# Splitting weight chunks in one piece of 2048 columns instead of two of 1024, in a two-layer encoder trunk

## The chip, the cores and the metric

The kernel runs on one core of one Trainium2 chip. The metric is device time in microseconds for one execution. A core has TensorE (PE: matrix products), VectorE (DVE), ScalarE (ACT), GpSimd (POOL), and SyncE (SP), whose queue issues all DMA transfers here. Times of whole runs are medians; a trace comes from one profiled execution.

## The reference

The input x is 256 tokens of 2048 float32 values, with one conditioning vector c. Each of two layers has a token mixer and a SwiGLU feed-forward part, and each part is wrapped in the same frame:

```python
for layer in range(2):
    shift1, scale1, gate1, shift2, scale2, gate2 = split(silu(c) @ ada_w[layer] + ada_b[layer], 6)
    h = x * (1 + scale1) + shift1
    out = mixer_ab(h) if layer == 0 else mixer_cd(h)
    x = layer_norm(ALPHA * x + (1 + gate1) * out)
    h = x * (1 + scale2) + shift2
    x = layer_norm(ALPHA * x + (1 + gate2) * ((silu(h @ w_gate) * (h @ w_up)) @ w_down))
```

mixer_ab is a gated linear recurrence beside a spatial gating unit, mixer_cd is stick-breaking attention beside multi-scale pooling; both have one input projection (2048 to 4096 columns) and one output projection (2048 to 2048). The feed-forward width is 5632. The conditioning product silu(c) @ ada_w has 12,288 outputs a layer, each a dot product of length 2048. Nearly all of the work is products of 256 tokens with float32 weights that are read once.

## The kernel before

Weights come from memory as raw chunks of 1 MB: 128 partitions by four blocks of 512 columns, 2048 columns in all, where the four blocks are four slices of the contracted dimension. A chunk is split into a high part h (the value rounded to the product format) and a low part l (the rest): `split` (lines 81 to 86) lets ScalarE copy w into h (line 84) and VectorE subtract h from w into l (line 85). `load_w` (line 144) splits a chunk in two halves of 1024 columns. TensorE then computes, for each block of 512 columns, xh·h, xh·l and xl·h (lines 161 to 163, the function `products`): 24 products for a chunk with both groups of 128 tokens, 12 for a half. xh and xl are the same split of the activations.

The h pieces and the l pieces have pools of four buffers each (lines 52 and 53), so four halves, two chunks, exist at a time. A buffer can be written again when the last product that reads it is done. Raw chunks share a pool of four buffers (line 51) with the tiles of ada_w, also 1 MB each.

`linear` (line 181) runs a projection: for each group of output blocks, for each chunk of the contracted dimension, load, split, multiply, and at the last chunk evacuate the sums. After each chunk it calls a pump, which issues conditioning work at a rate: 1.0 ada_w tile a chunk up to and including part of the first feed-forward, then 0.65, 0.84 and 0.2. `ada_dot` (line 94) loads one tile of ada_w and lets VectorE multiply it with silu(c) and sum along the columns, 1024 columns at a time into two partial sums; `ada_final` (line 102) adds the two partial sums, adds the bias, and folds in norm weights.

In the program's head (lines 523 to 570) the input projection's first columns are made as the conditioning terms arrive: each of 16 steps needs two ada_w dot products before its products. The feed-forward of layer 0 starts with three passes that go through one chunk of the contracted dimension for ten output blocks each (rate 1.0, with an addition on VectorE for each output), so that the later quarters of its input can be conditioned meanwhile. At the end of each output or down projection a hand-off (`close`, line 326) follows: the last sums, the norm, and the first products of the next stage, in a written order.

Outside the hand-offs a scheduler places the instructions of each engine in a fixed order when the program is built. An engine works its queue strictly in that order.

Of the kernel before, what the change touches and what calls it, by code (L numbers as in the profile page):

```python
# [7 lines left out]
F32 = mybir.dt.float32  # L8
F32R = mybir.dt.float32r
AF = mybir.ActivationFunctionType  # L10
ALU = mybir.AluOpType
PSUM = bass.MemoryType.PSUM

P = 128
# [4 lines left out]
NB = 512  # L19
# [23 lines left out]
def trunk_kernel(ctx, tc, I, out):  # L43
    nc = tc.nc
    V, A, G, T = nc.vector, nc.scalar, nc.gpsimd, nc.tensor

    def pool(name, bufs, **kw):
        return ctx.enter_context(tc.tile_pool(name=name, bufs=bufs, **kw))

    const = pool("const", 1)  # L50
    p_raw = pool("raw", 4)
    p_h = pool("wh", 4)
    p_l = pool("wl", 4)
    p_xs = pool("xs", 4)
    p_res = pool("res", 1)
    p_row = pool("rows", 1)
    p_t = pool("tmp", 2)
    p_d = pool("dram", 2, space=bass.MemoryType.DRAM)

    silc = const.tile([P, D], F32, name="silc")  # L60
# [14 lines left out]
    def vc(name, i, n=1):  # L75
        a = _VEC[name][0] + i
        return vec[:, a:a + n]
# [3 lines left out]
    def split(src, hp, lp, shape, hname, lname):  # L81
        h = hp.tile(shape, F32R, name=hname)
        l = lp.tile(shape, F32R, name=lname)
        A.activation(h, src, AF.Copy)  # L84
        mark["v"] = V.tensor_tensor(l, src, h, op=ALU.subtract)  # L85
        return h, l
# [7 lines left out]
    def ada_dot(acc, l, idx, kb):  # L94
        w = p_raw.tile([P, D], F32, name="w")
        nc.sync.dma_start(w, I["ada_w"][l, idx, kb])
        for hf in range(2):
            cs = slice(hf * 1024, hf * 1024 + 1024)
            V.scalar_tensor_tensor(w[:, cs], w[:, cs], 1.0, silc[:, cs], op0=ALU.mult, op1=ALU.mult,  # L99
                                   accum_out=acc[:, hf:hf + 1])  # L100

    def ada_final(acc, l, s, nm, idx, k0, n):
        m = mods[l, s, nm][:, k0:k0 + n]
        V.tensor_tensor(m, acc[:, :, 0], acc[:, :, 1], op=ALU.add)
        bias = vc("ab", (6 * l + idx) * KB + k0, n)
        if nm == "sh":
            V.tensor_tensor(m, m, bias, op=ALU.add)
        else:
            V.scalar_tensor_tensor(m, m, 1.0, bias, op0=ALU.add, op1=ALU.add)
        ln = 2 * l + s - 1  # L110
        if nm == "sh" and ln >= 0:
            sc = mods[l, s, "sc"][:, k0:k0 + n]
            t4 = p_t.tile([P, n], F32, name="t4")
            V.tensor_tensor(t4, vc("nb", ln * 16 + k0, n), sc, op=ALU.mult)
            V.tensor_tensor(m, m, t4, op=ALU.add)
            V.tensor_tensor(sc, sc, vc("ng", ln * 16 + k0, n), op=ALU.mult)

    def ada_tiles(l, s, part, q, n=CH):
        for nm, idx in (("sc", 3 * s + 1), ("sh", 3 * s)) if part == "s" else (("gt", 3 * s + 2),):
            acc = p_t.tile([P, n, 2], F32, name="ga")  # L120
            for j in range(n):
                ada_dot(acc[:, j], l, idx, n * q + j)
                if j == n - 1:
                    ada_final(acc, l, s, nm, idx, n * q, n)
                yield

    def chain(units):
        for u in units:
            if callable(u):
                u()  # L130
            else:
                yield from ada_tiles(*u)
# [6 lines left out]
    def load_raw(src):  # L139
        w = p_raw.tile([P, 4, NB], F32, name="w")  # L140
        nc.sync.dma_start(w, src)
        return w

    def load_w(src):
        w = load_raw(src)
        return [split(w[:, 2 * hf:2 * hf + 2], p_h, p_l, [P, 2, NB], "h", "l") for hf in range(2)]

    def products32(bk, x, w, tb, halves, first, last):
        ts = slice(tb * P, tb * P + P)
# [31 lines left out]
    def linear(groups, chunks, wsrc, stat, evac, after=None, pump=None, opened=None, close=None,  # L181
# [3 lines left out]
        for gi, group in enumerate(groups):  # L185
            banks = opened if gi == 0 and opened is not None else {}
            for ci, ch in enumerate(chunks):
# [11 lines left out]
                if close is not None and left == 1:  # L199
                    close(group, {nb: load_w(wsrc(nb, ch)) for nb in group}, banks, st, evac)  # L200
                    break
                for nb in group:
                    xr = raw(gi, ci, nb) if raw is not None else None
                    hl = load_w(wsrc(nb, ch)) if xr is None else load_raw(wsrc(nb, ch))
                    flush(mark["v"])
                    for hf in range(2):
                        for tb in range(2):
                            if first and hf == 0:
                                banks[nb, tb] = acc_bank()
                            if xr is None:  # L210
                                products(banks[nb, tb], st, hl, tb, (hf,), first, last)
                            else:
                                products32(banks[nb, tb], xr, hl, tb, (hf,), first, last)
                    if last:
                        for tb in range(2):
                            evac(nb, tb, banks[nb, tb])
                    if pump is not None and not (close is not None and left <= QUIET):
                        pump()
# [277 lines left out]
    def mixer_ab(pump):  # L496
        with ExitStack() as st:
# [15 lines left out]
            with tc.tile_pool(name="pshead", bufs=1, space=PSUM) as p8, tc.tile_pool(name="hraw", bufs=3) as p_hr:  # L513
# [3 lines left out]
                def stream(nb, ch):  # L517
                    hl = load_w(src(nb, ch))
                    for tb in range(2):
                        bk = p8.tile([P, NB], F32, name=f"hs{tb}")  # L520
                        products(bk, xs[ch], hl, tb, range(2), True, True)
                        d = dst[nb][:, tb]
                        if ch == 0:
                            A.activation(d, bk, AF.Copy)
                        else:
                            V.tensor_tensor(d, d, bk, op=ALU.add)
                        if ch == 3:
                            A.activation(d, d, AF.Gelu_apprx_tanh)

                spread(silc, 4, lambda i: p8.tile([P, NB], F32, name=f"hs{i % 2}"), AF.Silu)  # L530
                for kb in range(KB):
                    ch, k = divmod(kb, CH)
                    xt = y[ch]
                    ada = ada_tiles(0, 0, "s", kb, 1)
                    if kb == 0:
                        drain(ada)
                    if kb == 4:
                        rate = lru_rate()
                    if k == 0:
                        nc.sync.dma_start(xt, I["xT"][:, 4 * ch:4 * ch + 4])  # L540
                    w = p_hr.tile([P, 3, NB], F32, name="w")
                    nc.sync.dma_start(w, I["w_hd"][kb])
                    drain(ada)
                    sc, sh = (mods[0, 0, n][:, kb:kb + 1] for n in ("sc", "sh"))
                    V.tensor_scalar(xt[:, k], xt[:, k], sc, sh, op0=ALU.mult, op1=ALU.add)  # L545
                    for i, (nb, tb) in enumerate(head):
                        T.matmul(banks[nb, tb], xt[:, k, tb * P:tb * P + P], w[:, i // 2], start=kb == 0, stop=kb == KB - 1)  # L547
                    if k == 3:
                        xs.append(xs_split(xt))
                    elif ch > 0:  # L550
                        stream((7, 4, 5)[k], ch - 1)
# [363 lines left out]
```

## Time and profile before

| what | value |
|---|---|
| timed runs | 2183.04 us median of 3 (2177.11 to 2186.82) |
| profiled execution, span from first to last instruction | 2175.9 us (the page gives no time beside the span) |
| TensorE busy | 2111.6 us, 97% |
| VectorE busy | 1618.6 us, 74% |
| ScalarE busy | 966.5 us, 44% |
| moved by DMA | 601.20 MB, mean 276 GB/s |

How to read it: an engine that is busy for most of the span is not at its peak for that reason, because a product's record is longer than the distance to the next one. Where engines work in a loop, the distance between starts is the cost of an instruction, and the record's length is the time until its result is there. The chain of waits says which work ended last at each step; only what lies in that chain can shorten the run.

### The profile page before, as it was taken

How to read it: one execution, taken by the hardware profiler on the slowest of the kernel's cores; microseconds unless marked ns; L12 is line 12 of the kernel's file. 1: busy time of each engine (PE TensorE's matmuls, PEld its weight loads, DVE VectorE, ACT ScalarE, POOL GpSimd, SP SyncE). 2: the span in 40 equal slices, each digit the busy share in tenths (PEclk: the TensorE clock that was granted, in tenths of full speed). 3: DMA queues.
4: the chain of work that ended last, by engine and by line, in shares of the span. 5: the costliest groups of instructions: out<-in, count | busy, mean ns of one | idle time of the engine just before them, and what ended most of it. 6: DMA issues, size and time to landing. Idle time of an engine off the chain costs nothing.

```text
span 2175.9 us, 24074 instructions
## 1 busy us (share of the span) xinstructions
PE 2111.6 (97%) x9124; PEld 1666.4 (77%) x9124; DVE 1618.6 (74%) x2202; ACT 966.5 (44%) x1124; POOL 31.5 (1%) x55
## 2 busy tenths in 40 slices
PE   7989999999999999999999999999999999999996
PEld 3556767887888888888868777868888888888885
DVE  7778988899977788889779977666555555555656
ACT  1215733544544445444444556354444444444442
POOL 0000000000000000000000011000000000000000
PEclk9999999999999999999999999999999999999998
DMA  9987787988888888888858877646676666555552
GB/s 399 388 322 267 303 329 297 341 325 336 301 314 312 322 330 322 335 319 312 319 217 311 324 267 292 261 173 221 230 271 229 222 226 233 208 203 193 194 194 91
DMA packets 84747, 601.20 MB, mean 276 GB/s; under 512 B 9444, under 2 KB 9876, under 8 KB 13846
## 3 DMA queue, kind: packets, MB, share of 16 engines
q1 hardware_dynamic: 84630, 599.67, 73.7%
q8 instruction: 71, 1.16, 0.2%
q14 instruction: 46, 0.37, 0.1%
HBM read 597.51 MB, written 2.12 MB: 276 GB/s over the span
## 4 chain that ended last, share of the span: by engine, by line
PE 85%; DVE 9%; ACT 2%; DMA 2%; issue 1%; POOL 1%; SPq 0%; DVEq 0%; ACTq 0%; POOLq 0%
PE acc L162 25%; PE acc L163 25%; PE acc L161 24%; DVE w L99 3%; PE hd L547 3%; PE acc L152 3%; DVE l L85 2%; PE aux L228 2%; DMA w<-in_ada_w 1%; PE hs L162 1%; PE hs L163 1%; PE hs L161 1%; DMA w<-in_w_cd 0%; ACT h L84 0%; POOL z L736 0%
## 5 line engine op out<-in xcount | busy, mean ns | idle before, releaser
L85 DVE TENSOR_TENSOR l<-w,h 128x1024 fp32r<-128x1024 f32 x676 | 822.9, 1223 | 421.4 <-ACT h L84 420.1
L84 ACT ACTIVATE h<-w 128x1024 fp32r<-128x1024 f32 x676 | 711.6, 1059 | 862.0 <-PE acc L163 689.4
L162 PE MATMUL acc<-l,xh 128*128 128x512 f32 x2608 | 1019.2, 391 | 6.2 <-DVE l L85 5.8
L161 PE MATMUL acc<-h,xh 128*128 128x512 f32 x2608 | 1018.2, 392 | 5.9 <-ACT xh L318 4.5
L163 PE MATMUL acc<-h,xl 128*128 128x512 f32 x2608 | 1018.3, 391 | 0.0
L162 PEld LDWEIGHTS acc<-l,xh 128*128 128x128 f32 x2608 | 489.8, 188 | 112.4 <-DVE l L85 11.8
L161 PEld LDWEIGHTS acc<-h,xh 128*128 128x128 f32 x2608 | 489.5, 188 | 108.2 <-ACT xh L318 5.5
L163 PEld LDWEIGHTS acc<-h,xl 128*128 128x128 f32 x2608 | 489.8, 188 | 100.4 <-DVE xl L319 0.3
L99 DVE SCALAR_TENSOR_TENSOR w<-w,silc 128x1024 f32<-128x1024 f32 x384 | 459.0, 1219 | 18.0 <-DMA w<-in_ada_w 15.6
L547 PE MATMUL hd<-w,y 128*128 128x512 f32 x192 | 93.8, 642 | 20.7 <-DVE y L545 20.7
L547 PEld LDWEIGHTS hd<-w,y 128*128 128x128 f32 x192 | 38.4, 205 | 72.7 <-issue 43.2
L85 DVE TENSOR_TENSOR xl<-hid,xh 128x1024 fp32r<-128x1024 f32 x44 | 53.9, 1224 | 34.2 <-ACT xh L84 33.6
L84 ACT ACTIVATE xh<-hid 128x1024 fp32r<-128x1024 f32 x44 | 46.8, 1063 | 63.0 <-PE acc L162 63.0
L152 PE MATMUL acc<-w,hx 128*128 128x512 f32 x96 | 43.1, 599 | 2.8 <-ACT hx L313 2.7
L161 PE MATMUL hs<-h,xh 128*128 128x512 f32 x96 | 40.9, 428 | 0.0
L162 PE MATMUL hs<-l,xh 128*128 128x512 f32 x96 | 39.0, 406 | 0.0
L163 PE MATMUL hs<-h,xl 128*128 128x512 f32 x96 | 38.0, 396 | 0.0
L84 ACT ACTIVATE xh<-y 128x1024 fp32r<-128x1024 f32 x12 | 12.7, 1058 | 56.6 <-DVE y L545 48.6
L152 PEld LDWEIGHTS acc<-w,hx 128*128 128x128 f32 x96 | 17.6, 190 | 23.4 <-issue 17.5
L99 DVE DVE_READ_ACCUMULATOR w<-w,silc 128x1 f32 x384 | 31.3, 82 | 0.0
L152 PE MATMUL acc<-w,y 128*128 128x512 f32 x64 | 28.5, 592 | 0.0
L427 DVE TENSOR_TENSOR hid<-hid,acc 128x512 f32<-128x512 f32 x40 | 27.2, 683 | 1.5 <-PE acc L163 1.4
(207 smaller groups left out, 851.4 us busy)
## 6 DMA issues: line engine op xcount, KB each, us to landing
w<-in_ada_w SPq DMA_DIRECT2D x192, 1024.0 KB, 5.1
w<-in_wg SPq DMA_DIRECT2D x88, 1024.0 KB, 5.2
w<-in_wu SPq DMA_DIRECT2D x88, 1024.0 KB, 5.1
w<-in_wd SPq DMA_DIRECT2D x88, 1024.0 KB, 4.9
w<-in_w_cd SPq DMA_DIRECT2D x32, 1024.0 KB, 6.2
w<-in_w_ab SPq DMA_DIRECT2D x20, 1024.0 KB, 5.2
w<-in_w_ab_out SPq DMA_DIRECT2D x16, 1024.0 KB, 7.0
w<-in_w_cd_out SPq DMA_DIRECT2D x16, 1024.0 KB, 6.7
```

The source lines that it names most:

```text
L84: A.activation(h, src, AF.Copy)
L85: mark["v"] = V.tensor_tensor(l, src, h, op=ALU.subtract)
L99: V.scalar_tensor_tensor(w[:, cs], w[:, cs], 1.0, silc[:, cs], op0=ALU.mult, op1=ALU.mult, accum_out=acc[:, hf:hf + 1])
L152: T.matmul(bk, x[:, k, ts], w[:, k], start=first and k == 0, stop=last and k == 3)
L161: T.matmul(bk, xh[:, k, ts], h[:, j], start=first and k == 0, stop=False)
L162: T.matmul(bk, xh[:, k, ts], l[:, j], start=False, stop=False)
L163: T.matmul(bk, xl[:, k, ts], h[:, j], start=False, stop=last and k == 3)
L228: T.transpose(pt[:, i], src[:, i * P:(i + 1) * P], ident)
L427: V.tensor_tensor(part(nb, tb), part(nb, tb), bk, op=ALU.add)
L547: T.matmul(banks[nb, tb], xt[:, k, tb * P:tb * P + P], w[:, i // 2], start=kb == 0, stop=kb == KB - 1)
```

## The change

The pools for h and l get two buffers each, and a buffer holds a whole chunk of 2048 columns. `load_w` splits a chunk in one call, so with one ScalarE copy and one VectorE subtraction of 2048 columns, and hands the two halves of the result to the same products as before. The memory used is the same. `ada_dot` is one VectorE instruction of 2048 columns with one sum, and `ada_final` no longer adds two partial sums.

```diff
-    p_h = pool("wh", 4)
-    p_l = pool("wl", 4)
+    p_h = pool("wh", 2)
+    p_l = pool("wl", 2)
...
-        for hf in range(2):
-            cs = slice(hf * 1024, hf * 1024 + 1024)
-            V.scalar_tensor_tensor(w[:, cs], w[:, cs], 1.0, silc[:, cs], op0=ALU.mult, op1=ALU.mult,
-                                   accum_out=acc[:, hf:hf + 1])
+        V.scalar_tensor_tensor(w, w, 1.0, silc, op0=ALU.mult, op1=ALU.mult, accum_out=acc)
...
-        V.tensor_tensor(m, acc[:, :, 0], acc[:, :, 1], op=ALU.add)
...
-            V.tensor_tensor(m, m, bias, op=ALU.add)
+            V.tensor_tensor(m, acc, bias, op=ALU.add)
...
-            V.scalar_tensor_tensor(m, m, 1.0, bias, op0=ALU.add, op1=ALU.add)
+            V.scalar_tensor_tensor(m, acc, 1.0, bias, op0=ALU.add, op1=ALU.add)
...
-            acc = p_t.tile([P, n, 2], F32, name="ga")
+            acc = p_t.tile([P, n], F32, name="ga")
...
-                ada_dot(acc[:, j], l, idx, n * q + j)
+                ada_dot(acc[:, j:j + 1], l, idx, n * q + j)
...
-        return [split(w[:, 2 * hf:2 * hf + 2], p_h, p_l, [P, 2, NB], "h", "l") for hf in range(2)]
+        h, l = split(w, p_h, p_l, [P, 4, NB], "h", "l")
+        return [(h[:, 2 * hf:2 * hf + 2], l[:, 2 * hf:2 * hf + 2]) for hf in range(2)]
```

The order of the instructions moves with it. First VectorE's queue in the input projection of layer 1, around chunks 177 to 180 of the 338 that are split, in the kernel before. L99 is a dot product, L85 a subtraction (l from w and h), L375 and L376 work on the residual x that is only due later, L104 and L109 finish a group of four dot products.

```order
L99 SCALAR_TENSOR_TENSOR w,ga<-w,silc 128x1024 x2
L375 TENSOR_TENSOR x<-x,rg 128x512
L104 TENSOR_TENSOR m11sc<-ga 128x4
L375 TENSOR_TENSOR x<-x,rg 128x512
L109 SCALAR_TENSOR_TENSOR m11sc<-m11sc,vec 128x4
L376 TENSOR_TENSOR x<-x,rb 128x512 x2
L85 TENSOR_TENSOR l<-w,h 128x1024 x2
L99 SCALAR_TENSOR_TENSOR w,ga<-w,silc 128x1024 x2
L375 TENSOR_TENSOR x<-x,rg 128x512 x2
L376 TENSOR_TENSOR x<-x,rb 128x512 x2
L85 TENSOR_TENSOR l<-w,h 128x1024 x2
```

Between two pairs of subtractions stand two dot products of 1024 columns with the residual additions of one chunk. The same place in the changed kernel, where lines behind the change are three lower (L372 and L373 are the residual work, L97 the dot product, L105 the first finishing step).

```order
L97 SCALAR_TENSOR_TENSOR w,ga<-w,silc 128x2048
L372 TENSOR_TENSOR x<-x,rg 128x512
L105 SCALAR_TENSOR_TENSOR m11sc<-ga,vec 128x4
L372 TENSOR_TENSOR x<-x,rg 128x512
L373 TENSOR_TENSOR x<-x,rb 128x512 x2
L85 TENSOR_TENSOR l<-w,h 128x2048
L97 SCALAR_TENSOR_TENSOR w,ga<-w,silc 128x2048
L372 TENSOR_TENSOR x<-x,rg 128x512 x2
L373 TENSOR_TENSOR x<-x,rb 128x512 x2
L85 TENSOR_TENSOR l<-w,h 128x2048
```

Each pair of 1024 wide instructions has become one of 2048, one small instruction is gone, and the sequence is the same.

Second, ScalarE's queue at the hand-off from the down projection of layer 0 to layer 1, in the kernel before. L84 is the copy of weights (h) or of hidden values (xh), L313 makes the scaled inputs hx and t of the next stage, L318 copies them.

```order
L84 ACTIVATE xh<-hid 128x1024
L84 ACTIVATE h<-w 128x1024 x17
L313 ACTIVATE hx_7814<-aux,m10sh,m10sc 128x128 x4
L313 ACTIVATE t_7843<-aux,m10sh,m10sc 128x128 x4
L318 ACTIVATE xh<-t_7843 128x4x128
```

Two of the 17 half copies make a chunk, so the odd one at the start closes a chunk begun above. The same place in the changed kernel (L310 and L315 are the scaled inputs and their copy).

```order
L84 ACTIVATE xh<-hid 128x1024
L84 ACTIVATE h<-w 128x2048 x9
L310 ACTIVATE hx_6962<-aux,m10sh,m10sc 128x128 x4
L310 ACTIVATE t_6991<-aux,m10sh,m10sc 128x128 x4
L315 ACTIVATE xh<-t_6991 128x4x128
```

Before, the last four of the 17 half copies belong to two chunks of the next stage; after, the last two of the 9 whole ones do. Both stand ahead of hx. SP's queue carries the same transfers; a few loads of norm rows, pooling weights and gate rows have changed places with their neighbours.

## Rows read from the trace of the kernel before

**Rows 1.** The page's head: span; busy us, share, instructions by engine.
```profile
span 2175.9 us, 24074 instructions
PE 2111.6 (97%) x9124; PEld 1666.4 (77%) x9124; DVE 1618.6 (74%) x2202; ACT 966.5 (44%) x1124; POOL 31.5 (1%) x55
```

**Rows 2.** Chain that ended last: the page's by engine, the view's own by line.
```profile
PE 85%; DVE 9%; ACT 2%; DMA 2%; issue 1%; POOL 1%; SPq 0%; DVEq 0%; ACTq 0%; POOLq 0%
by line: PE acc L162 24.6%; PE acc L163 24.5%; PE acc L161 24.3%; DVE w L99 3.2%; PE hd L547 3.0%; PE acc L152 2.9%; DVE l L85 2.4%; PE aux L228 1.9%; issue 1.5%; DMA w<-in_ada_w 1.2%; PE hs L162 0.9%; PE hs L163 0.9%; PE hs L161 0.9%; DMA 
```

**Rows 3.** Stretches: length, busy us (count) PE PEld DVE ACT POOL, clock, DMA.
```profile
1460.00:2156.00 696.00, 696.00 (x3113) 575.89 (x3112) 403.70 (x405) 308.80 (x314) 0.00 (x0) 1.00 0.59 212
```

**Rows 4.** Stretches, TensorE alone: length, busy us (instructions), clock, DMA.
```profile
520.00:530.00 10.00, 9.64 (x41) 1.00 0.94 367
1200.00:1210.00 10.00, 10.00 (x46) 1.00 0.94 338
```

**Rows 5.** Timeline, gate and up projection: start, length, engine, line, instruction, idle before.
```profile
1611.06 0.39 PE L161 MATMUL acc<-h,xh 128*128 128x512 f32 x1
...
1613.78 0.39 PE L161 MATMUL acc<-h,xh 128*128 128x512 f32 x1
1613.98 1.06 ACT L84 ACTIVATE h<-w 128x1024 fp32r<-128x1024 f32 x1 [1.66 <-PE acc L163]
...
1615.07 1.23 DVE L85 TENSOR_TENSOR l<-w,h 128x1024 fp32r<-128x1024 f32 x1 [1.50 <-ACT h L84]
```

**Rows 6.** Groups by shape: count, busy us, mean ns, idle before.
```profile
L319 DVE TENSOR_TENSOR xl<-t,xh 128x512 fp32r<-128x512 f32 x18 | 12.4, 688 | 20.2 <-ACT xh L318 20.1
...
L318 ACT ACTIVATE xh<-t 128x512 fp32r<-128x512 f32 x18 | 11.5, 640 | 0.2
```

**Rows 7.** The page's costliest groups: count, busy us, mean ns, idle before.
```profile
L85 DVE TENSOR_TENSOR l<-w,h 128x1024 fp32r<-128x1024 f32 x676 | 822.9, 1223 | 421.4 <-ACT h L84 420.1
L84 ACT ACTIVATE h<-w 128x1024 fp32r<-128x1024 f32 x676 | 711.6, 1059 | 862.0 <-PE acc L163 689.4
```

**Rows 8.** Timeline of VectorE in the head.
```profile
80.36 1.22 DVE L99 SCALAR_TENSOR_TENSOR w<-w,silc 128x1024 f32<-128x1024 f32 x1
...
81.50 1.22 DVE L99 SCALAR_TENSOR_TENSOR w<-w,silc 128x1024 f32<-128x1024 f32 x1
...
82.76 0.16 DVE L104 TENSOR_TENSOR m00sc<-ga 128x1 f32<-128x1 f32 x1
82.95 0.16 DVE L109 SCALAR_TENSOR_TENSOR m00sc<-m00sc,vec 128x1 f32<-128x1 f32 x1
```

**Rows 9.** Chain in the output projection of layer 0: start, us, what.
```profile
288.31 1.07 ACT h L84
...
290.68 0.50 PE acc L162
...
341.80 1.24 DVE l L85
```

**Rows 10.** Timeline of VectorE, layer 1.
```profile
1198.58 1.29 DVE L375 TENSOR_TENSOR x<-x,rg 128x512 f32<-128x512 f32 x2
```

**Rows 11.** Groups by shape, 1100 to 1300, TensorE.
```profile
L695 PE MATMUL aux<-pp,rg 128*128 128x256 f32 x32 | 7.4, 385 | 0.3 <-DVE pp L691 0.3
```

**Rows 12.** Timelines of ScalarE and TensorE at the second hand-off.
```profile
1105.15 1.06 ACT L84 ACTIVATE h<-w 128x1024 fp32r<-128x1024 f32 x1 [0.30 <-DVE x L269]
1106.12 1.49 ACT L313 ACTIVATE hx<-aux,m10sh,m10sc 128x128 f32<-128x128 f32 x4
...
1106.61 7.13 PE L152 MATMUL acc<-w,hx 128*128 128x512 f32 x16 [1.06 <-ACT hx L313]
```

**Rows 13.** Timelines of SP and ScalarE, output projection of layer 0.
```profile
291.79 0.33 SPq L141 DMA_DIRECT2D w<-in_w_ab_out  x1
...
302.69 0.33 SPq L141 DMA_DIRECT2D w<-in_w_ab_out  x1
...
299.21 2.01 ACT L84 ACTIVATE h<-w 128x1024 fp32r<-128x1024 f32 x2 [2.83 <-DMA w<-in_w_ab_out]
```

## The prediction

> **What bounds the kernel now.** I read the page's busy shares first, then the chain of waits, then stretches of TensorE, then single loops. TensorE is busy nearly all of the 2175.9 us span, VectorE three quarters, ScalarE under half [rows 1]. The chain that ended last runs 85% through TensorE and 9% through VectorE [rows 2]. In the longest stretch, 1460 to 2156, TensorE has no idle at all [rows 3]: a saving on VectorE or ScalarE is worth nothing there. At full pace TensorE starts 46 matmuls in 10 us (1200 to 1210), and in the worst 10 us of the middle stage 41 [rows 4]. So the change can gain only where VectorE stands in the chain: the head, the stage up to 365, and short pieces after it. Everywhere else the question is whether it makes TensorE wait. The clock that the profile grants is 1.00 in these stretches, so it is no term.
>
> **The loop that the change alters.** Twelve matmuls, one half of a chunk, take 1613.78 - 1611.06 = 2.72 us, a chunk 5.44. ScalarE starts the next copy 0.20 after TensorE has gone on to the next half (1613.98), the copy takes 1.06, VectorE's subtraction starts 0.03 later and takes 1.23: done 2.52 after the half was given back [rows 5]. Before, with four half buffers, this half is wanted three halves later, 8.16 us, and its low part only with the second matmul, 0.23 later: about 5.8 us to spare.
>
> After, a buffer comes back only when the whole chunk is done, and is wanted one chunk later. No 2048 wide instruction stands in the trace, so I bound it. From the 512 wide rows [rows 6] and the 1024 wide ones [rows 7], one doubling more gives 1.06 + 2 x (1.06 - 0.64) = 1.90 on ScalarE and 1.22 + 2 x (1.22 - 0.69) = 2.29 on VectorE; at most they cost two of the old ones, 2.12 and 2.45. I take 1.90 and 2.29, since the same kind of instruction gives both points of the line. Done at 0.20 + 1.90 + 0.03 + 2.29 + 0.05 = 4.47, wanted at 5.67: 1.2 us to spare (0.8 at the upper bound). So no chunk waits by itself, but the reserve against bursts falls from 5.8 to 1.2.
>
> **What is saved.** On VectorE two old dot products start 1.14 apart (80.36, 81.50), and the sum of the two halves costs 0.19 until the next small instruction (82.76 to 82.95) [rows 8]. One 2048 wide instruction holds VectorE 1.14 + 2 x 0.54 = 2.22 where two held 2.28: 0.06 a pair, for 338 splits and 192 dot products 32 us, and some 80 sums at 0.19 (one per accumulator group) 15 us. Of the 1619 us of VectorE only what lies in the chain counts. Bounds: nothing, and the saving on all that the chain holds, 3.2% of the span in dot products (70 us, 30 pairs, at 0.25 each 7.6) and 2.4% in subtractions (52 us, 23 pairs, 1.4) [rows 2]: 9 us.
>
> **Sum, stage by stage.**
> Head (to 200 us): each step of the first projection needs two dot products and their sums one after the other, 0.5 us less a step. About seven of the sixteen steps have TensorE waiting for them (four at the start, three where a group of four ends, counted in the chain): -3.5.
>
> 200 to 365: transfers pace the weights. When TensorE is already waiting, the halves no longer overlap: at 288.31 the copy starts, and TensorE goes on at 290.68 [rows 9]; with the whole chunk it needs 1.90 + 2.29 + 0.09 = 4.28 instead of 2.37: +1.9. The piece of the chain on VectorE that ends with the subtraction at 341.80 [rows 9] costs another 1.1 at its end, and its 13 merged pairs give back 1: +2 together.
>
> Middle (365 to 690): VectorE must do a split, a dot product and two additions a chunk. Two 512 wide additions start 0.60 apart (1.29 for two) [rows 10]. Before 2.28 + 2.28 + 1.20 = 5.76, after 2.22 + 2.22 + 1.20 = 5.64, against TensorE's 5.44; only eight chunks of ten have a dot product. Before loses little, 5 starts of 46 in the worst slice [rows 4]; after is 0.12 cheaper a chunk but has less reserve. With the two later places where four residual instructions meet a dot product: +1.
>
> 1165 to 1420: the two orders shown for VectorE carry the same work. Between two splits it may hold 5.44 - 2.22 = 3.22 without loss, and 1.2 in all may pile up. The intervals in a row are 2.40 + 2.22 = 4.62, then 2.40, then 4.77 (0.15 for a small one), then 4.62: 0.2 lost, 0.4 left over, then 0.75 and 1.4 lost: +2.35. Before, the same four sum to about 4 us over, under its 5.8, and [rows 4] shows 46 starts there. The two intervals behind, with the pooling, are longer (6.2 and 7.2), but TensorE has the pooling matmuls (16 of a group of 32 with 7.4 us [rows 11]) and sixteen transposes there, so I count 1.3 for its waits, and 0.85 for the attention: +4.5.
>
> Hand-offs: at 1105.15 ScalarE starts its last half copy, at 1106.12 the scaled inputs, and TensorE goes on at 1106.61 [rows 12]. The order after keeps both copies ahead; the second is released by the same matmul but takes 1.90: +0.85, at two of the three hand-offs: +1.7.
>
> Stages that TensorE fills, and the tail: 0. The cover is the 1.2 us; in the down projection a copy of hidden values as long as an old half copy, about 1 us, stands ahead of the split, in the gate projection one activation. At the upper bound of the 2048 wide costs the first would lose 0.1 a chunk pair, 5 us in all; below zero nothing can come here, as TensorE has no idle. SP issues the same transfers, and the moved row loads change places with others that wait for buffers anyway.
>
> Sum: -3.5 + 2 + 1 + 4.5 + 1.7 = +5.7 on 2175.9, so 2182. The page gives no other time for its execution; the median of the timed runs lies 7.1 above the span, so I predict 2189.
>
> **Rivals.**
> Faster, because VectorE's chain is worth its whole saving and no burst reaches TensorE: -9, so 2174. For it: VectorE stands in the chain for 9% of the span, 196 us. Against: the 85% on TensorE [rows 2].
>
> Slower, by the lost reserve. The place is VectorE's queue, where a split stands behind a burst; it decides from 1.2 us over 3.22 a chunk. If TensorE's own extra work does not hide the bursts between 1165 and 1420 they cost about 12, the middle 5, the hidden copies of the down projections 5, the stage to 365 2, hand-offs 1.7, less 3.5 for the head: +22, so 2205. For it: bursts of 4.6 and more follow each other in the order. Against: they fall where pooling and attention fill TensorE. The Trainium skill, Perfetto Trace Analysis, section Optimizing Scalar/DVE Operations, sides with it: larger operations help when the engine is saturated, but "If Scalar/Vector aren't saturated, but are causing bubbles on other engines, breaking up instructions may allow work to be completed sooner." VectorE is at 74% and the copy at 288.31 fits that rule; a reader of the rule alone would take the 2205.
>
> Slower, by the transfers. A raw buffer is given back later. In the loop issued at 291.79, landed at 299.21, issued again at 302.69 [rows 13] the part after landing is 3.48; whole it is 1.90 + 2.29 + 0.06 = 4.25: 0.39 a chunk, if the loop of four raw buffers binds. With two loads a chunk in about 46 chunks that is 18, with the other terms but the 2 of the stage to 365 +22, again 2205. For it: the copy at 299.21 had waited 2.83 us for its transfer [rows 13]. Against: a load that queues less lands sooner, so part of it comes back.
>
> **How the numbers follow.** Forecast 0.45, faster rival 0.15, lost reserve 0.25, transfers 0.15. A change under 0.5%, 11 us, can't be told from none, so faster is under 2172, slower over 2194. Faster: under half of its rival and a little of the forecast, 0.14. Slower: nine tenths of the two slow rivals and the upper end of the forecast, 0.40. Same: 0.46. The forecast's own range is 2178 to 2200; the range with the rivals 2171 to 2213.
>
> **What would show it.** After: splits of about 1.90 and 2.29; TensorE without idle from 1460 on; new idle behind the subtraction between 1165 and 1240, 3 to 6 us in all; the hand-offs later by under 1 us each; the head 3 us shorter. I am wrong if TensorE waits for the subtraction in stretches where VectorE has time, if ScalarE's waits for transfers turn into idle of TensorE by the chunk, or if the 2048 wide instructions lie outside their bounds.

## The result

The changed kernel takes 2210.15 us (median of 4 runs, 2206.69 to 2212.84) against 2180.4 of the kernel before in the same session: a ratio of 1.013, 95% interval 1.0111 to 1.0149. It is 1.3% slower. The time lies inside the range of 2171 to 2213, but the likeliest case, 2189 with its own range of 2178 to 2200, did not come; nearest are the two slow rivals, the lost reserve and the transfers, both priced at 2205. Of the three outcomes, slower (chance 0.40) came and not same (0.46).

The page after: span and engines, the chain, the costliest groups (answering to [rows 1, 2, 7]).

```profile
span 2204.9 us, 22580 instructions
PE 2119.9 (96%) x9124; PEld 1667.9 (76%) x9124; DVE 1569.0 (71%) x1417; ACT 898.9 (41%) x777; POOL 35.9 (2%) x55
...
PE 83%; DVE 9%; ACT 3%; DMA 3%; issue 2%; POOL 1%; DVEq 0%; POOLq 0%; ACTq 0%
...
L85 DVE TENSOR_TENSOR l<-w,h 128x2048 fp32r<-128x2048 f32 x338 | 774.3, 2291 | 420.2 <-ACT h L84 419.5
...
L84 ACT ACTIVATE h<-w 128x2048 fp32r<-128x2048 f32 x338 | 647.4, 1915 | 802.1 <-PE acc L160 685.8
...
L97 DVE SCALAR_TENSOR_TENSOR w<-w,silc 128x2048 f32<-128x2048 f32 x192 | 438.9, 2287 | 52.8 <-DMA w<-in_ada_w 49.3
```

VectorE is busy for 50 us less and ScalarE for 68 us less, and the run is longer. The prices are those estimated: 1.915 for the copy (1.90), 2.291 for the subtraction (2.29). What failed is where they were set against the need of TensorE.

**Where the 29 us arise.** TensorE has 9124 products and transposes in each trace, so the start of the n-th in one can be set against the start of the n-th in the other. The two orders differ in at least 857 places, but at every stage's end in the table below the n-th product is the same one in both. The table gives how much later each stage of the changed kernel ends than it did before, less what it was already late when the stage began.

| stage, by the times of before | us | forecast |
|---|---|---|
| head, to 200 | -3.7 | -3.5 |
| output projection of layer 0, to 350 | +3.6 | +2 (to 365) |
| first hand-off, 350 to 400 | +8.7 | 0.85 at two of the three hand-offs |
| feed-forward of layer 0, 400 to 1090 | +7.3 | +1, residual included |
| second hand-off, 1090 to 1150 | +4.1 | as the first |
| input projection, attention, 1150 to 1404 | +2.9 | +4.5 |
| third hand-off, 1404 to 1465 | +4.1 | as the first |
| feed-forward of layer 1, 1465 to 2140 | +0.4 | 0 |
| last chunks, 2140 to the end | +1.7 | 0 |

The three hand-offs and the last chunks make 18.5 of the 29.0, where 1.7 was forecast.

**The hand-off.** First TensorE in the kernel before, at the first two products of the second of the last two chunks; then TensorE, ScalarE and VectorE of the changed kernel at the same place, the second hand-off.

```profile
1096.79 0.39 PE L161 MATMUL acc<-h,xh 128*128 128x512 f32 x1
1097.02 0.39 PE L162 MATMUL acc<-l,xh 128*128 128x512 f32 x1
```

```profile
1109.71 0.39 PE L160 MATMUL acc<-h,xl 128*128 128x512 f32 x1
1109.94 0.39 PE L158 MATMUL acc<-h,xh 128*128 128x512 f32 x1
...
1112.66 0.39 PE L158 MATMUL acc<-h,xh 128*128 128x512 f32 x1
1114.43 0.50 PE L159 MATMUL acc<-l,xh 128*128 128x512 f32 x1 [1.39 <-DVE l L85]
```
```profile
1110.14 1.92 ACT L84 ACTIVATE h<-w 128x2048 fp32r<-128x2048 f32 x1 [3.52 <-PE acc L160]
...
1122.70 1.91 ACT L84 ACTIVATE h<-w 128x2048 fp32r<-128x2048 f32 x1 [0.81 <-PE acc L160]
1124.52 1.49 ACT L310 ACTIVATE hx<-aux,m10sh,m10sc 128x128 f32<-128x128 f32 x4
```
```profile
1112.09 2.29 DVE L85 TENSOR_TENSOR l<-w,h 128x2048 fp32r<-128x2048 f32 x1 [3.15 <-ACT h L84]
```

The chunk ahead of the last two ends with the product at 1109.71 and frees its buffers; at 1109.94 the first of the two begins. But `close` (line 326) takes the two last chunks by token group: twelve products of one, then twelve of the other. So the second, which goes into the freed buffers, is wanted after 12 x 0.2267 = 2.72 us, its low part after 2.95, and not after 5.67 as in the body of a projection. Its buffer needs 0.20 + 1.92 + 0.03 + 2.29 + 0.05 = 4.49: late by 1.54. Measured against the pitch (0.2267 a product): 1114.43 instead of 1112.89, 1.54. Before, the same product started without a wait (1097.02). The same wait of 1.39 idle stands at all four places (358.02, 1114.43, 1435.65, 2180.32); at the last pair of chunks it stands in the stretch that answers to [rows 3], where TensorE had no idle: there TensorE now has 696.00 - 694.61 = 1.39 idle.

```profile
1488.00:2184.00 696.00, 694.61 (x3104) 573.62 (x3103) 393.92 (x255) 276.70 (x177) 0.00 (x0) 1.00 0.58 212
```

The forecast term of the hand-offs is there as it was worked out: hx starts behind a 1.91 copy, and TensorE goes on after 1.91 idle where [rows 12] show 1.06: 0.85, at the second and the third.

```profile
1125.02 7.13 PE L149 MATMUL acc<-w,hx 128*128 128x512 f32 x16 [1.91 <-ACT hx L310]
...
1446.24 7.13 PE L149 MATMUL acc<-w,hx 128*128 128x512 f32 x16 [1.91 <-ACT hx L310]
```

**The first hand-off** loses more. VectorE there, before and after, then TensorE after:

```profile
371.03 0.26 DVE L289 BATCH_NORM_AGGREGATE mv<-st 128x2 f32<-128x24 f32 x1
371.33 0.15 DVE L291 TENSOR_SCALAR rs<-mv 128x1 f32<-128x1 f32 x1
```
```profile
374.84 0.26 DVE L286 BATCH_NORM_AGGREGATE mv<-st 128x2 f32<-128x24 f32 x1
375.01 2.23 DVE L97 SCALAR_TENSOR_TENSOR w<-w,silc 128x2048 f32<-128x2048 f32 x1
...
377.17 0.15 DVE L288 TENSOR_SCALAR rs<-mv 128x1 f32<-128x1 f32 x1
```
```profile
378.74 1.94 PE L225 MATMUL aux<-ident,x 128*128 128x128 f32 x8 [3.50 <-DVE x L301]
```

The scheduler has put a whole dot product between the aggregate of the norm and its next step, rs, at both token groups (363.24 and 375.01). Before, two half dot products stood in the second norm too, but ahead of its last statistics, and none in the first. This stands in the changed order of instructions and I did not look there: I had compared the hand-off on ScalarE alone.

**The clock.** In the first profile of before TensorE's granted clock is at its full level (2.4 GHz) from 181 us to 2164. In the changed kernel it falls to one half (1.2 GHz) in the stretches below, each behind idle at a hand-off (and once at 319); the same products then start 0.43 apart instead of 0.23.

```profile
377.40:384.20 6.80, 5.46 (x13) 3.33 (x14) 3.28 (x7) 2.54 (x6) 0.55 (x1) 0.50 0.61 255
1135.20:1138.50 3.30, 3.30 (x11) 2.69 (x10) 2.05 (x4) 0.06 (x1) 0.00 (x0) 0.50 0.55 231
1456.00:1459.30 3.30, 3.23 (x9) 2.55 (x10) 1.61 (x3) 0.01 (x1) 0.00 (x0) 0.50 0.00 0
```

At the second hand-off the products in that stretch lose 0.2 each, with the transposes 1.6 in all. There 1.54 + 0.85 + 1.6 = 4.0 of the 4.1. At the first hand-off the longer stretch costs 2.3.

**The middle.** TensorE's waits for the subtraction between the first two hand-offs, before and after (us in total, times, longest).

```profile
PE acc L162 <- DVE l L85: 0.8, 3, 0.4
```
```profile
PE acc L159 <- DVE l L85: 5.9, 5, 2.6
```

The longest of the five: VectorE in the feed-forward of layer 0, then TensorE.

```profile
708.85 2.29 DVE L97 SCALAR_TENSOR_TENSOR w<-w,silc 128x2048 f32<-128x2048 f32 x1 [5.17 <-DMA w<-in_ada_w]
...
711.07 4.49 DVE L85 TENSOR_TENSOR l<-w,h 128x2048 fp32r<-128x2048 f32 x2
```
```profile
713.41 0.50 PE L159 MATMUL acc<-l,xh 128*128 128x512 f32 x1 [2.62 <-DVE l L85]
```

VectorE waits 5.17 us for an ada_w tile while a split, its copy long done, stands behind the dot product. One more of the five (0.2 at 665.77) is of this kind. The other three (0.7 at 480.75, 1.2 at 531.74, 1.2 at 560.53; 3.1 together) are of another: there the split stands behind an addition of the three passes, and the addition waits for TensorE's own sums. VectorE, then TensorE:

```profile
528.79 0.69 DVE L424 TENSOR_TENSOR hid<-hid,acc 128x512 f32<-128x512 f32 x1 [1.18 <-PE acc L160]
529.39 2.29 DVE L85 TENSOR_TENSOR l<-w,h 128x2048 fp32r<-128x2048 f32 x1
```
```profile
531.74 0.50 PE L159 MATMUL acc<-l,xh 128*128 128x512 f32 x1 [1.17 <-DVE l L85]
```

The tiles do come later for VectorE than before: its dot products wait for them 49.3 us in the whole run, where they waited 15.6 in the first profile of before and 25.3 in the second (below).

```profile
DVE w L99 <- DMA w<-in_ada_w: 15.6, 18, 3.6
```
```profile
DVE w L97 <- DMA w<-in_ada_w: 49.3, 36, 7.4
```

### The profile page after: what moved, and what is told of

Read it like the earlier page. It is cut to its first block, busy times and chain, and to the rows that moved or that the text cites. A ratio compares the mean times of both kernels' runs of the same rounds, so it can differ in the third digit from the quotient of the medians.

```text
span 2204.9 us, 22580 instructions
## 1 busy us (share of the span) xinstructions
PE 2119.9 (96%) x9124; PEld 1667.9 (76%) x9124; DVE 1569.0 (71%) x1417; ACT 898.9 (41%) x777; POOL 35.9 (2%) x55
## 4 chain that ended last, share of the span: by engine, by line
PE 83%; DVE 9%; ACT 3%; DMA 3%; issue 2%; POOL 1%; DVEq 0%; POOLq 0%; ACTq 0%
PE acc L159 24%; PE acc L160 24%; PE acc L158 24%; DVE l L85 3%; DVE w L97 2%; PE hd L544 2%; PE acc L149 2%; PE aux L225 2%; DMA w<-in_ada_w 1%; ACT h L84 1%; PE hs L159 1%; PE hs L160 1%; PE hs L158 1%; DMA w<-in_w_ab_out 1%; POOL th L733 1%
## 5 line engine op out<-in xcount | busy, mean ns | idle before, releaser
L85 DVE TENSOR_TENSOR l<-w,h 128x2048 fp32r<-128x2048 f32 x338 | 774.3, 2291 | 420.2 <-ACT h L84 419.5
L84 ACT ACTIVATE h<-w 128x2048 fp32r<-128x2048 f32 x338 | 647.4, 1915 | 802.1 <-PE acc L160 685.8
L97 DVE SCALAR_TENSOR_TENSOR w<-w,silc 128x2048 f32<-128x2048 f32 x192 | 438.9, 2287 | 52.8 <-DMA w<-in_ada_w 49.3
L84 ACT ACTIVATE xh<-hid 128x1024 fp32r<-128x1024 f32 x44 | 46.8, 1063 | 144.5 <-PE acc L159 144.5
L85 DVE TENSOR_TENSOR xl<-hid,xh 128x1024 fp32r<-128x1024 f32 x44 | 53.9, 1224 | 53.1 <-ACT xh L84 53.1
L395 ACT ACTIVATE sg<-acc 128x512 f32<-128x512 f32 x34 | 20.4, 600 | 46.9 <-PE acc L160 46.9
L149 PEld LDWEIGHTS acc<-w,hx 128*128 128x128 f32 x96 | 18.4, 198 | 25.9 <-issue 18.5
L84 ACT ACTIVATE xh<-y 128x1024 fp32r<-128x1024 f32 x12 | 12.7, 1058 | 53.4 <-DVE y L542 44.0
L316 DVE TENSOR_TENSOR xl<-t,xh 128x512 fp32r<-128x512 f32 x18 | 12.4, 689 | 27.0 <-ACT xh L315 27.0
```

Source lines behind the costliest of these rows:

```text
L97: V.scalar_tensor_tensor(w, w, 1.0, silc, op0=ALU.mult, op1=ALU.mult, accum_out=acc)
L149: T.matmul(bk, x[:, k, ts], w[:, k], start=first and k == 0, stop=last and k == 3)
L395: A.activation(sg, bk, AF.Silu)
```

## The experiments

All edits are to the changed kernel unless the text says otherwise. Lags are against the first profile of before, by stage as above. Every edit also changes the order that the scheduler makes, so the total of a run tests an edit together with its order; a wait at one place can be followed by itself.

**The kernel before, once more.** No edit.

> The kernel before, profiled once more. Theory: whether the granted clock falls behind the waits of a hand-off varies from execution to execution, so this one has one to three half-speed stretches between 200 and 2150 us, each worth 1.4 to 1.7 us at the hand-offs, and a span of 2177 to 2183. Rival (the changed kernel's longer waits alone make the clock fall): none, as in the first profile, and a span within 1 us of 2175.9 there.

Measured: span 2181.7, one half-speed stretch behind the second hand-off.

```profile
1121.40:1124.80 3.40, 3.40 (x11) 2.73 (x10) 2.75 (x5) 0.99 (x3) 0.00 (x0) 0.50 0.12 51
```

It loses 1.4 there, with the waits that the first profile had. So a fall behind a hand-off is partly chance, and the clock is no clean part of the 29. The first profile was a fortunate one: a run takes some 1.8 more than its span (2183.39 and 2181.7 here, 2206.69 and 2204.9 after), so its 2175.9 lies 2 to 5 us under the medians of before (2180.1 to 2183.04 less 1.8), and the 7.1 that I put between span and time was mostly that. This execution is also 1.8 later at 200 us, so the head's 3.7 is uncertain by as much or more.

**Only the dot products wide.**

```diff
-    p_h = pool("wh", 2)
-    p_l = pool("wl", 2)
+    p_h = pool("wh", 4)
+    p_l = pool("wl", 4)
...
-        h, l = split(w, p_h, p_l, [P, 4, NB], "h", "l")
-        return [(h[:, 2 * hf:2 * hf + 2], l[:, 2 * hf:2 * hf + 2]) for hf in range(2)]
+        return [split(w[:, 2 * hf:2 * hf + 2], p_h, p_l, [P, 2, NB], "h", "l") for hf in range(2)]
```

> Only the dot products are 2048 wide; splits as before (1024 wide, four half buffers). Theory (the loss is made by the whole-chunk splits at the hand-offs): the head keeps its 3.7 us, the hand-offs stand as before, so 2 to 5 us under the kernel before, 2175 to 2179. Rival (wide dot products stand ahead of the splits on VectorE and hold them up): 5 to 15 us over before.

Measured: 2183.17, ratio 1.0008 (0.9998 to 1.0018). Neither: no loss, and no gain. The head is 4.7 ahead at 200 us; 3.3 is given back between 400 and 1090 (2.5 of it between 640 and 800) and 4.4 between 1150 and 1404, and two half-speed stretches behind hand-offs take 3.1. The wide dot product alone does not explain the result.

**Only the splits wide.** The other half of the change: `ada_dot` and `ada_final` as in the kernel before.

> Only the splits are 2048 wide with two whole buffers; dot products as before, 1024 wide in two sums. Theory: the loss at the hand-offs stays and the head gives nothing back, so 24 to 33 us over before, 2204 to 2213; idle of 1.39 on TensorE before the low product of the second of the last two chunks, four times. Rival (wide dot products): at most 15 us over before.

Measured: 2214.84, ratio 1.0147 (1.0126 to 1.0168): 32 over before, within the 24 to 33 expected; the four waits are there. With the splits alone the loss is as large, though not at the same places: the first hand-off costs 1.7 instead of 8.7 (one half dot product stands between the aggregate and rs of the first norm, none in the second), and the stage to 350 and the middle lose more.

**The same buffers, filled in two instructions.**

```diff
-        h, l = split(w, p_h, p_l, [P, 4, NB], "h", "l")
-        return [(h[:, 2 * hf:2 * hf + 2], l[:, 2 * hf:2 * hf + 2]) for hf in range(2)]
+        h = p_h.tile([P, 4, NB], F32R, name="h")
+        l = p_l.tile([P, 4, NB], F32R, name="l")
+        hl = [(h[:, 2 * hf:2 * hf + 2], l[:, 2 * hf:2 * hf + 2]) for hf in range(2)]
+        for hf in range(2):
+            s = w[:, 2 * hf:2 * hf + 2]
+            A.activation(hl[hf][0], s, AF.Copy)
+            mark["v"] = V.tensor_tensor(hl[hf][1], s, hl[hf][0], op=ALU.subtract)
+        return hl
```

> Whole-chunk buffers, two each as in the changed kernel, but filled by two 1024 wide instructions on each engine; dot products 2048 wide. Theory (a whole buffer is harmless if its first half is ready 2.6 us after release instead of 4.5, since the hand-off wants it after 2.95): no 1.39 idle at the hand-offs, no fall of the granted clock behind them, 3 us under to 5 over before, 2177 to 2185. Rival (that a whole buffer comes back late is enough by itself): 15 to 25 over before.

Measured: 2183.08, ratio 1.0004 (0.9993 to 1.0016). Two whole buffers instead of four halves cost nothing that can be measured; the 27 us between this kernel and the changed one go with the width of the instructions that fill them. No idle at the four places. (One expectation missed: a half-speed stretch follows at the second hand-off all the same, with the waits of before: chance again.) The rule that I had set beside the rival holds here: the Trainium skill, Perfetto Trace Analysis, section Optimizing Scalar/DVE Operations, says that where VectorE or ScalarE is not saturated but makes others wait, breaking up its instructions may let work complete sooner. VectorE is at 71%, and halving brings the whole loss back.

**One copy, two subtractions; two copies, one subtraction.**

```diff
-        for hf in range(2):
-            s = w[:, 2 * hf:2 * hf + 2]
-            A.activation(hl[hf][0], s, AF.Copy)
-            mark["v"] = V.tensor_tensor(hl[hf][1], s, hl[hf][0], op=ALU.subtract)
+        A.activation(h, w, AF.Copy)
+        for hf in range(2):
+            mark["v"] = V.tensor_tensor(hl[hf][1], w[:, 2 * hf:2 * hf + 2], hl[hf][0], op=ALU.subtract)
```
```diff
+        for hf in range(2):
+            A.activation(hl[hf][0], w[:, 2 * hf:2 * hf + 2], AF.Copy)
+        mark["v"] = V.tensor_tensor(l, w, h, op=ALU.subtract)
```

(both against the kernel with two instructions; the second replaces the same loop)

> The changed kernel with one 2048 wide copy on ScalarE and two 1024 wide subtractions on VectorE for a chunk. Theory (the time from the release of a whole buffer to its first low half decides): 0.20 + 1.92 + 0.03 + 1.23 + 0.05 = 3.43 against 2.95 wanted, so a wait of 0.3 to 0.5 at each of the four hand-offs instead of 1.39; losses between 200 and 800 us between those of two instructions (about 2) and of one (about 10 without the hand-off): 2185 to 2197. Rival (ScalarE's width decides): waits of 1.39 as in the changed kernel, 2205 to 2211.

> The changed kernel with two 1024 wide copies on ScalarE and one 2048 wide subtraction on VectorE. Theory: first low half 0.20 + 1.06 + 1.0 + 0.03 + 2.29 + 0.05 = 4.6 after the release, so waits of 1.4 to 1.7 at the four hand-offs and the same losses as in the changed kernel: 2204 to 2213. Rival (ScalarE's width decides): waits under 0.6 and 2185 to 2197.

TensorE at the second hand-off, first with two subtractions, then with two copies:

```profile
1104.89 0.50 PE L164 MATMUL acc<-l,xh 128*128 128x512 f32 x1 [0.37 <-DVE l L147]
```
```profile
1127.45 0.50 PE L164 MATMUL acc<-l,xh 128*128 128x512 f32 x1 [1.48 <-DVE l L147]
```

Set against the pitch these are 0.53 and 1.64 later, where 3.43 - 2.95 = 0.48 and 4.63 - 2.95 = 1.68 were worked out ahead: with none with two instructions, as expected, and 1.54 of 1.54 in the changed kernel, worked out afterwards, the sum from release to first low half holds at four points. Two subtractions: 2193.70, ratio 1.0057 (1.0041 to 1.0074), as expected. Two copies: 2221.59, ratio 1.0184 (1.0166 to 1.0201), 9 above what was expected. Some 12 us arise between 100 and 200 us, where TensorE waits up to 2.8 for a split that stands behind norm statistics in this kernel's order; why the scheduler orders it so was not followed up.

**Only the hand-off's chunks in halves.** `load_w` gets a flag, set where `close` is called, with which it fills its two buffers by the loop of two instructions.

```diff
-                    close(group, {nb: load_w(wsrc(nb, ch)) for nb in group}, banks, st, evac)
+                    close(group, {nb: load_w(wsrc(nb, ch), True) for nb in group}, banks, st, evac)
```

> The changed kernel, but the two chunks that a hand-off works off are split by two 1024 wide instructions each (into the same whole buffers). Theory: the four waits of 1.55 go, 6.2 us, and with them the fall of the clock behind two hand-offs, some 3, and most of the 8.6 of the first hand-off, where no dot product stands between the aggregate and the next step any more: 2193 to 2199. If the waits alone count: 2204. Rival (the lost reserve in the middle of the run, spread over many chunks): within 2 us of the changed kernel, 2208 to 2211.

Measured: 2202.08, ratio 1.0095 (1.0081 to 1.0109). The four waits are gone: the first hand-off costs 0.2 (no dot product stands in its norm here), the second 1.0, the last chunks 0; the third 4.1, hx and two half-speed stretches. But 400 to 1090 now loses 13.1 instead of 7.3, and 200 to 350 5.7 instead of 3.6, so that 8 of the expected 11 to 17 is left, nearest to the 2204 of the waits alone. The saving at the hand-offs is shown; so is a loss of the middle that is there without it.

**The dot products behind the norm.**

```diff
-        V.scalar_tensor_tensor(w, w, 1.0, silc, op0=ALU.mult, op1=ALU.mult, accum_out=acc)
+        with ExitStack() as st:
+            if "late" in mark:
+                st.enter_context(tc.issue_after(mark["n"].ins))
+            V.scalar_tensor_tensor(w, w, 1.0, silc, op0=ALU.mult, op1=ALU.mult, accum_out=acc)
...
-        V.tensor_scalar(rs, mv[:, 1:2], EPS, None, op0=ALU.add)
+        mark["n"] = V.tensor_scalar(rs, mv[:, 1:2], EPS, None, op0=ALU.add)
...
     drain_all(early)
+    mark["late"] = True
```

> The changed kernel, with the dot products of the feed-forward and later stages placed behind the last norm's rs on VectorE, so that none stands between the aggregate and rs of the first hand-off. Theory: of the 8.65 us that the first hand-off costs in the changed kernel, 1.5 (the wait for the whole-chunk split) and at most 1 stay; 5 to 7 go, clock fall included, so 2203 to 2206. Rival (the order is harmless, the late second pair of splits makes the 3.5 us wait): under 2 us, 2208 to 2211.

Measured: 2208.91, ratio 1.0126 (1.0107 to 1.0145). The place is as expected: 8.7 becomes 1.7, the wait of 1.54 and little more, so the dot product in the norm (and the clock behind it) made the other 7. The total is not, and lies where the rival put it: 400 to 1090 loses 14.0 in this trace. Here and in the kernel with the hand-off's chunks in halves, the two that keep wide splits and wide dot products and free the first hand-off, the middle loses 6 to 7 more than in the changed kernel; one half-speed stretch at 715 is part of it in both traces. That the dot products moved out of the hand-off are the ones in the way later is likely, and not shown.

**Thin dot products, after and before.** Behind the mixer of layer 0 each dot product takes 64 of its 2048 columns (the rest is left out); all transfers stay.

```diff
+        n = 64 if "late" in mark else D
-        V.scalar_tensor_tensor(w, w, 1.0, silc, op0=ALU.mult, op1=ALU.mult, accum_out=acc)
+        V.scalar_tensor_tensor(w[:, 0:n], w[:, 0:n], 1.0, silc[:, 0:n], op0=ALU.mult, op1=ALU.mult, accum_out=acc)
```

> The changed kernel, with the dot products behind the first hand-off cut to 64 of their 2048 columns (the rest of these sums is left out); their transfers stay. To be read against the next kernel. Theory (the losses between 400 and 1100 us are splits that stand behind dot products and additions in VectorE's queue): from 400 to 1090 TensorE loses under 2 us against the next kernel, where the changed kernel loses 7.3 against the one before; in all 6 to 13 us over the next kernel. Rival (raw buffers come back late and transfers with them): 5 to 9 us between 400 and 1090, in all 14 to 25.

> The kernel before, with the dot products behind the first hand-off cut to 32 of the 1024 columns of each half (the rest of these sums is left out); the control of the kernel ahead. Both theories: 0 to 4 us under before, since VectorE is the bound only around 500 to 530 us.

Measured: 2189.91 and 2176.17. Between 400 and 1090 the first loses 0.9 against the second, where the changed kernel loses 7.3, with the same bytes moved, and VectorE waits for tiles as long as in the changed kernel (53.5 us). So tiles that come late do not by themselves make the loss: it takes the time of whole dot products in VectorE's queue as well. Whether these would cost as much with tiles that come in time was not tested. TensorE's waits for the subtraction are 2.1 in the first and 2.0 in the second, again behind additions. In all 13.7 by the medians, a little over the expected 13 and just under the rival's 14; that is 16 less than the changed kernel's 29.8, of which the two profiles put 6.6 at the first hand-off and 6.4 between 400 and 1090. The first hand-off costs 2.1 although a whole split stands in its second norm as in the changed kernel, so the dot products made the rest. The four waits and hx stay, and 200 to 350, where the dot products are still whole, keeps 4.8.

**Wide dot products in the head alone**, on the kernel before.

```diff
+        if wide:
+            V.scalar_tensor_tensor(w, w, 1.0, silc, op0=ALU.mult, op1=ALU.mult, accum_out=acc[:, 0:1])
+            return
...
-                ada_dot(acc[:, j], l, idx, n * q + j)
+                ada_dot(acc[:, j], l, idx, n * q + j, n == 1)
```

(`ada_final` skips the sum of the halves there.)

> The kernel before with 2048 wide dot products in the head alone (the 32 of the first projection's conditioning), everything else as before. Theory: the head's 3.5 to 4.7 us stay and nothing is lost later: 2177 to 2180, ratio 0.998 to 0.9985. Rival (what the head gains the stage to 365 gives back, since transfers pace it): within 1 us of before.

Measured: 2179.91 against 2180.52, ratio 0.9991 (0.9981 to 1.0001). The trace is 2.5 ahead at 200 us and 0.8 at 350: most is given back by the stage that transfers pace. It can't be told from no change, as the rival had it, so no version here that does all the work beats the kernel before.

| kernel | head | to 350 | 1st hand-off | 400 to 1090 | 2nd | 1150 to 1404 | 3rd | end |
|---|---|---|---|---|---|---|---|---|
| before, once more | 1.8 | 0.6 | 0.0 | 1.9 | 1.4 | 0.2 | 0.0 | 0.0 |
| changed | -3.7 | 3.6 | 8.7 | 7.3 | 4.1 | 2.9 | 4.1 | 1.7 |
| dots wide | -4.7 | 0.7 | 0.0 | 3.3 | 1.7 | 4.4 | 1.4 | 0.0 |
| splits wide | -0.4 | 7.4 | 1.7 | 11.0 | 5.5 | 7.6 | 4.3 | 1.7 |
| two instructions | -3.9 | 0.9 | 0.1 | 9.3 | 1.8 | 0.3 | 0.0 | 0.0 |
| two subtractions | -0.9 | 1.1 | 1.0 | 6.2 | 3.0 | 3.2 | 1.7 | 0.7 |
| two copies | 10.3 | 5.8 | 3.2 | 9.6 | 5.4 | 7.4 | 3.6 | 1.8 |
| hand-off in halves | -0.7 | 5.7 | 0.2 | 13.1 | 1.0 | 3.4 | 4.1 | 0.0 |
| dots behind norm | -1.2 | 5.7 | 1.7 | 14.0 | 2.7 | 2.2 | 4.3 | 1.7 |
| thin, after less before | -3.8 | 4.8 | 2.1 | 0.9 | 3.3 | 1.4 | 2.4 | 1.7 |
| head wide | -2.5 | 1.7 | 0.0 | 0.1 | -0.1 | 0.4 | 0.0 | 0.0 |

Each row is one execution; single waits of the middle come and go (the two instructions lose 4.5 at one late tile in 9.3, in an execution 3.9 above their median), so differences under some 5 us there mean little. The end repeats to 0.1, and the hand-offs, clock aside, to a few tenths.

## Why the prediction was right and wrong

The sum was +5.7 on the span, and 29.0 came. The stated range held only because the slow rivals were in it.

- Prices: right (1.915 and 2.291, the four points of the sum above).
- Head -3.5: -3.7 in this profile. That this one profile hits it is partly luck: four kernels with the same order of instructions in the head (changed, hand-off in halves, dots behind norm, thin after) lie at -3.7, -0.7, -1.2 and -2.4 against the first profile of before, and three with the head of before at 0, 1.8 and 1.4. The means differ by 3.1, so the term is right within the scatter.
- 200 to 365, +2: 3.6 by 350. The piece at 341.80 in [rows 9] cost the 1.1 forecast: TensorE waits there as below (second line). Of the 1.9 for the chunk at 288.31 only 0.6 came: its price is there (copy at 284.07, TensorE goes on at 288.37, 4.30 against the 4.28 worked out), but the copy now starts earlier against TensorE, whose wait grew from 0.46 to 1.05. The rest is a split on VectorE: with a 2048 wide subtraction the stage loses 3.6 to 7.4, with two halves about 1.

```profile
288.37 0.50 PE L159 MATMUL acc<-l,xh 128*128 128x512 f32 x1 [1.05 <-DVE l L85]
...
342.95 0.50 PE L159 MATMUL acc<-l,xh 128*128 128x512 f32 x1 [1.33 <-DVE l L85]
```

- Hand-offs +1.7: **this step failed.** The 0.85 of hx came twice as forecast. What failed is the sentence "no chunk waits by itself": a buffer "is wanted one chunk later" is true where a chunk's 24 products run in one piece, and `close` runs the last two by token group, 12 and 12. Four waits of 1.54, 6.2 us, followed from the rows and lines I had. The first of the signs of being wrong came with them: TensorE waits for the subtraction where VectorE has time (it stood idle for 3.15 ahead of the one at 1112.09). Beside it I read the order of the hand-off on ScalarE and not on VectorE, where a dot product had moved in between the aggregate and rs of each of the two norms: some 7 us with the clock behind them.
- Middle +1: 7.3. The mechanism is the lost reserve of 1.2 and bursts in VectorE's queue, named but priced for the residual work; what came were splits that stand behind a dot product waiting for its tile (2.8 of 5.9 us of waits) and behind additions waiting for TensorE (3.1). Cutting the dot products takes the loss to 0.9. The size is that of one execution: two instructions for a chunk lose 9.3 there in theirs and nothing in their median.
- 1165 to 1420, +4.5: 2.9, the VectorE part too large and the attention part too small. The idle behind the subtraction that was to be the sign, 3 to 6 us between 1165 and 1240, is 1.4 in two waits (0.35 at 1231.79, 1.08 at 1238.62); TensorE's waits for GpSimd in the attention grew by 1.9, from 5.8 to 7.7, where 0.85 was set.
- From 1460: no idle, as forecast, but for the last pair of chunks.
- The clock, called no term: behind idle of the hand-offs it is one, of 1.4 to 1.6 each time that it falls at the second and third and 2.3 at the first hand-off of the changed kernel, in executions of both kernels.
- The rivals: the gain did not come. The transfers by themselves fell where they were tested; late tiles have a part in the middle. Both slow rivals priced the result best, 2205. The lost reserve laid 12 us between 1165 and 1420 and 5 in the down projections, where 2.9 and 0.4 came.

## What to carry to other kernels

When instructions that fill a ring are made wider, work out the time from a buffer's release to its first usable part, and set it against the shortest distance between release and need in the program, not the usual one: the ends of loops, where work is taken in another order, decide. Here buffers could be merged at no cost as long as they were filled in pieces. A wide instruction that waits for a transfer on an in-order engine blocks what stands behind it, so read the new order on every engine at the places where a short dependent chain is in the path.

## What the runs showed of the hardware

- VectorE's 2048 wide instructions take 2.29 us each, the dot product with its sum as long as the subtraction; ScalarE's copy takes 1.92. From 1024 to 2048 columns they grow by 1.07 and 0.86, about twice what they grow from 512 [rows 6, 7].
- TensorE's granted clock falls to one half behind the idle of a hand-off in one execution and not in another of the same kernel: after the same waits of 1.06 and 2.26 us it stayed full in the first profile of before and fell in the second. With two subtractions it stayed full behind longer waits, of 1.96 and 2.26.
- Two traces of the same kernel differ by 5.8 us in span (2175.9 and 2181.7), 1.8 of it in the head and 1.4 in one such stretch: one profile is no measure for a term of 2 us. In the head, four traces of one order of instructions lie 3.0 apart.
